# A float32 transpose through TensorE: when stores are issued, and the order of copies into freed regions

## The chip, the cores and the metric

The kernel runs on one core of a Trainium2 chip. The metric is the device time of one execution in microseconds (us). Every profile shown is that of one execution; times inside it are counted from the start of its span.

## The reference

```
def reference(x):          # x: 8192 x 8192, float32
    return np.transpose(x)
```

268.4 MB are read from HBM and 268.4 MB are written to it.

## The kernel before

**Tiling.** The input is cut into two stripes of 4096 columns, and each stripe into 64 chunks of 128 rows: `chunks` has T = 128 entries (s, c), stripe by stripe. A chunk is one load of 2 MB (128 rows x 4096 floats) into one of NIN = 3 input buffers `in`. TensorE turns a chunk into 32 transposed tiles of 128x128, in eight groups q = 0 to 7 of four tiles. The groups 0 to 3 go to one half of PSUM (four banks, `pss[0]`), 4 to 7 to the other (`pss[1]`), so that the whole PSUM holds one chunk. ScalarE (ACT, e = 0) copies the first half to SBUF, VectorE (DVE, e = 1) the second.

**Windows and regions.** The copies go into `regs`, which has NREG = 9 regions of 2 MB. A group q gathers in one region the tiles of up to W = 8 successive chunks, so that a row of the output gets 8 x 128 floats, 4 KB, in one piece. This is the group's window. The windows are staggered: in each chunk one group's window closes (q = c mod 8), and its region is stored by one DMA (2 MB in the middle of the run, less at the start and the end; two pieces where a window spans the change of stripes). Eight windows are open, and one region is spare: a group that closed in chunk t opens its next window in chunk t+1, in the region that was freed by the store of chunk t-1. That store must have landed before the first copy into it.

**Semaphores.** TensorE waits for `s_ld` of its input buffer to come to 18 (line 113): 16 from the load's landing and one from each copying engine, `go`, which says that its half of PSUM has been emptied. It adds one to `s_pe` after every second group, four times a chunk. NH = 4 is the number of groups in a half. `s_st[r]` counts the landed stores of region r, and `s_cp[e]` the copies that closed a window.

**Order of the work around the change.** The queues are in order and the program of each engine is written out for all 128 chunks (TensorE has a loop). For a chunk t ScalarE's program is, before: for each run of groups that one instruction can copy, a wait for `s_pe` (line 222) and the copy (line 223); where a group opens a window in a region that was used before, a wait for `s_st` of that region stands ahead of all copies of the half (line 197); behind a copy that closes a window, a wait for `s_cp` and the store (`store`, lines 151 to 173, called at line 236). Stores of VectorE's half are issued by ScalarE too, behind its own copies, and wait for VectorE's `s_cp`. At last ScalarE waits until TensorE has finished chunk t and issues the load of chunk t+3 into the buffer that chunk t leaves free (lines 237 and 238). So all loads but the first three, and all stores, stand in ScalarE's one DMA queue, in the order store of t, load of t+3, store of t+1, load of t+4. The first three loads are issued by SyncE at the start.

The lines around the change, before:

```
nc.scalar.wait_ge(s_cp[e], count)                 # store: own copy done
...
if stored[r]:
    eng.wait_ge(s_st[r], 16 * stored[r])          # ahead of all copies of the half
...
if t + NIN < T:
    nc.scalar.wait_ge(s_pe, (t + 1) * NR // 2)    # TensorE done with chunk t
    load(t + NIN)
```

Of the kernel before, what the change touches and what calls it, by code (L numbers as in the profile page):

```python
# [40 lines left out]
def kernel(  # L41
# [13 lines left out]
    nc = tc.nc  # L55
# [8 lines left out]
    NR = S // B  # L64
# [5 lines left out]
    with tc.tile_critical():  # L70
        nc.alloc_sbuf_tensor("pad", [P, 32], dt)
        ident = nc.alloc_sbuf_tensor("ident", [P, P], dt).ap()
        ins = [nc.alloc_sbuf_tensor(f"in{k}", [P, J], dt).ap() for k in range(NIN)]
        SIZE = B * W * P
        regs = nc.alloc_sbuf_tensor("regs", [P, NREG * SIZE], dt).ap()
        NH = NR // 2
        pss = [nc.alloc_psum_tensor(f"ps{k}", [P, NH * B * P], dt).ap() for k in range(2)]

        s_id = nc.alloc_semaphore("s_id")
        s_ld = [nc.alloc_semaphore(f"s_ld{k}") for k in range(NIN)]  # L80
        s_st = [nc.alloc_semaphore(f"s_st{k}") for k in range(NREG)]
        s_pe = nc.alloc_semaphore("s_pe")
        s_cp = [nc.alloc_semaphore("s_cpa"), nc.alloc_semaphore("s_cpv")]

        nc.gpsimd.memset(ident, 0.0).then_inc(s_id, 1)  # L85
        nc.gpsimd.wait_ge(s_id, 1)
        nc.gpsimd.affine_select(  # L87
            out=ident,
            in_=ident,
            compare_op=mybir.AluOpType.not_equal,  # L90
            fill=1.0,
            base=0,
            pattern=[[-1, P]],
            channel_multiplier=1,
        ).then_inc(s_id, 1)
        nc.vector.sem_inc(s_ld[0], 1)
        nc.scalar.sem_inc(s_ld[0], 1)

        chunks = [(s, c) for s in range(M // J) for c in range(CH)]

        def load(t):
            s, c = chunks[t]
            (nc.sync if t < NIN else nc.scalar).dma_start(
                out=ins[t % NIN], in_=x[c * P:(c + 1) * P, s * J:(s + 1) * J]
            ).then_inc(s_ld[t % NIN], 16)

        def transposes(k):
            nc.tensor.sem_inc(s_ld[k], -18).wait_op(s_ld[k], 18, "sem-ge")  # L113
            for q in range(NR):
                e, g = divmod(q, NH)
                for b in range(B):
                    tr = nc.tensor.transpose(  # L117
                        pss[e][:, (g * B + b) * P:(g * B + b + 1) * P],
                        ins[k][:, q * B * P + b:(q + 1) * B * P - B + b + 1:B],
                        ident,  # L120
                    )
                if q % 2:
                    tr.then_inc(s_pe, 1)

        T = len(chunks)
        assert T % NIN == NIN - 1
        pe = [nc.tensor.engine]
        nc.tensor.wait_ge(s_id, 2)

        turn = nc.alloc_registers("turn", engines=pe)  # L130
        nc.regs_mov(turn, 0)
        nc.br("turns", engines=pe)
        with nc.body("turns", valid_engines=pe):
            now = nc.snap(turn, min_val=0, max_val=T // NIN)
            with nc.tensor.If(now > 0):
                transposes(NIN - 1)
            for k in range(NIN - 1):
                transposes(k)
            nc.regs_alu(turn, turn, 1, op=mybir.AluOpType.add)
            nc.tensor.br_lt(turn, T // NIN + 1, on_true="turns", on_false="done")  # L140
        nc.switch_bb("done")

        for t in range(NIN):
            load(t)

        copied = [0, 0]
        free = list(range(NREG))
        stored = [0] * NREG
        window = {}

        def store(q, e, count):
            t0, r, parts = window.pop(q)
            nc.scalar.wait_ge(s_cp[e], count)
            base = 0
            pieces = []
            for s, a, z in parts:
                rows = (z - a) * P
                j0 = s * J + q * B * P
                dst = out[j0:j0 + B * P, a * P:a * P + rows]
                dst = dst.rearrange("(q b) i -> q b i", q=P)  # L160
                src = regs[:, r * SIZE + base:r * SIZE + base + B * rows]
                base += B * rows
                pieces.append((rows, dst, src))
            for rows, dst, src in sorted(pieces, key=lambda v: -v[0]):
                if any(stored):
                    st = wide_dma(nc, nc.scalar, "qActDynamicHW", dst, src)
                else:
                    st = nc.scalar.dma_start(
                        out=dst, in_=src.rearrange("q (b i) -> q b i", b=B)
                    )  # L170
                st.then_inc(s_st[r], 16)
                stored[r] += 1
            free.append(r)

        def closes(w, t):
            t0, r, parts = w
            return t + 1 == t0 + sum(z - a for _, a, z in parts)

        for t, (s, c) in enumerate(chunks):
            for e in range(2):  # L180
                eng = (nc.scalar, nc.vector)[e]
                go = s_ld[(t + 1) % NIN]

                place = []
                for q in range(e * NH, (e + 1) * NH):
                    if q not in window:

                        span = (q - c) % W + 1  # L190
                        r = free.pop(0)
                        parts = [(s, c, min(c + span, CH))]
                        if c + span > CH and t + span < T:
                            parts.append((s + 1, 0, c + span - CH))
                        window[q] = (t, r, parts)
                        if stored[r]:
                            eng.wait_ge(s_st[r], 16 * stored[r])
                    t0, r, parts = window[q]
                    k = [p[0] for p in parts].index(s)
                    base = r * SIZE + B * P * sum(z - a for _, a, z in parts[:k])  # L200
                    _, a, z = parts[k]
                    place.append((base + (c - a) * P, (z - a) * P))

                runs = []
                for g in range(NH):
                    if runs:
                        u = runs[-1]
                        gap = place[g][0] - place[g - 1][0]
                        if place[g][1] == place[u[0]][1] and abs(gap) < 2 ** 15 and (
                            len(u) == 1 or gap == place[u[1]][0] - place[u[0]][0]  # L210
                        ):
                            u.append(g)
                            continue
                    runs.append([g])
                for u in runs:
                    off, dist = place[u[0]]
                    gap = place[u[-1]][0] - place[u[-2]][0] if len(u) > 1 else 0
                    dims = [list(regs.ap[0]), [gap, len(u)], [dist, B], [1, P]]
                    o = bass.AP(regs.tensor, regs.offset + off, dims)
                    i = pss[e][:, u[0] * B * P:(u[-1] + 1) * B * P]  # L220
                    i = i.rearrange("p (l b i) -> p l b i", b=B, i=P)
                    eng.wait_ge(s_pe, t * NH + (e * NH + u[-1]) // 2 + 1)  # L222
                    cp = nc.scalar.copy(out=o, in_=i) if e == 0 else nc.vector.tensor_copy(out=o, in_=i)  # L223
                    ends = [e * NH + g for g in u if closes(window[e * NH + g], t)]
                    if ends:
                        cp.then_inc(s_cp[e], 1)
                        copied[e] += 1
                    if u is runs[-1]:
                        if ends:
                            eng.wait_ge(s_cp[e], copied[e])  # L230
                            eng.sem_inc(go, 1)
                        else:
                            cp.then_inc(go, 1)
                    for q in ends:
                        store(q, e, copied[e])
            if t + NIN < T:
                nc.scalar.wait_ge(s_pe, (t + 1) * NR // 2)
                load(t + NIN)
        for r in range(NREG):
            nc.sync.wait_ge(s_st[r], 16 * stored[r])  # L240

# [29 lines left out]
```

## Time and profile before

| what | before |
|---|---|
| median of 3 runs | 1262.03 us (1261.98 to 1262.59) |
| profiled execution | 1262.98 us, of which the span is 1261.2 us |
| bytes read and written | 536.9 MB |
| DMA rate from 400 to 600 us | 430 GB/s |
| TensorE, ScalarE, VectorE busy | 59%, 20%, 24% |
| ACT-issued loads | 125, median 21.7 us from issue to landing |
| full stores | 114 of 2 MB, median 17.5 us from issue to landing |

The span runs from the first to the last instruction; the profiled execution took 1.8 us more than its span, and 0.95 us more than the median. "q10" is the DMA queue of ScalarE, "q1" that of SyncE, "q14" and "q8" carry instructions. A name with a small q behind an engine (ACTq, SPq, PEq) is that engine's sequencer: it issues a DMA or waits. In the table of windows the columns are the stretch and its length, then busy time and number of instructions of PE, PEld, DVE, ACT and POOL, then the granted TensorE clock, the DMA engines' share and the GB/s that they moved.

### The profile page before, as it was taken

The page shows a single profiled execution, that of the slowest core. Times are in us where ns is not written, and L with a number is a line of the kernel's source. Part 1 is how long each engine was busy: PE and PEld are TensorE (multiplying, and loading weights), DVE is VectorE, ACT ScalarE, POOL GpSimd, SP SyncE. Part 2 cuts the span into 40 slices and gives each one's busy share as a digit, 9 for nine tenths or more (in the row PEclk, how much of TensorE's full clock was granted, in tenths as well). Part 3 has the DMA queues.
Part 4 walks back from the last instruction along what each step waited for, and adds up shares of the span by engine and source line. Part 5 has one row for each costly group of instructions (what it writes and reads, how often), then busy time and mean ns, then how long its engine had stood idle before and what let it go on. Part 6 is the DMA issues. An engine that isn't in the chain of part 4 may idle for free. (4 is left out here: it accounts for less than half of the span.)

```text
span 1261.2 us, 9538 instructions
## 1 busy us (share of the span) xinstructions
PE 741.5 (59%) x4096; PEld 720.8 (57%) x4096; DVE 302.5 (24%) x250; ACT 252.8 (20%) x257; POOL 0.7 (0%) x6
## 2 busy tenths in 40 slices
PE   5665655656565655665566555656556555656561
PEld 5565655656565655665565555655556555655551
DVE  2322222222222222223222222222222222222220
ACT  3212121121111211122211221221111211121120
POOL 0000000000000000000000000000000000000000
PEclk9878677777868686777767777686777777686775
DMA  9999999999999999999999999999999999999998
GB/s 380 427 424 427 429 428 429 429 428 430 431 430 429 430 430 429 430 430 430 428 422 427 429 431 429 430 430 429 429 430 431 428 430 430 429 429 431 429 429 351
DMA packets 39273, 536.97 MB, mean 426 GB/s; under 512 B 4320, under 2 KB 4832, under 8 KB 6240
## 3 DMA queue, kind: packets, MB, share of 16 engines
q10 hardware_dynamic: 38832, 530.60, 98.9%
q1 hardware_dynamic: 432, 6.29, 1.2%
q14 instruction: 8, 0.07, 0.0%
q8 instruction: 1, 0.02, 0.0%
HBM read 268.44 MB, written 268.44 MB: 426 GB/s over the span
## 5 line engine op out<-in xcount | busy, mean ns | idle before, releaser
L117 PE MATMUL ps<-ident,in 128*128 128x128 f32 x4096 | 741.5, 363 | 492.6 <-PEq L113 492.6
L117 PEld LDWEIGHTS ps<-ident,in 128*128 128x128 f32 x4096 | 720.8, 220 | 513.0 <-issue 513.0
L223 DVE COPY regs<-ps 128x512 f32<-128x512 f32 (+3 forms) x250 | 302.5, 1246 | 933.1 <-PE ps L117 760.0
L223 ACT COPY regs<-ps 128x512 f32<-128x512 f32 (+3 forms) x256 | 251.5, 1015 | 980.5 <-PE ps L117 489.8
L223 ACT ACT_TABLE_LOAD x1 | 1.3, 1283 | 1.0 <-SPq L70 1.0
L87 POOL TENSOR_SCALAR_AFFINE_SELECT ident<-ident 128x128 f32<-128x128 f32 x1 | 0.3, 292 | 0.2 <-POOL ident L85 0.2
L85 POOL MEMSET ident<- 128x128 f32 x1 | 0.2, 204 | 0.5 <-SPq L70 0.5
L255 POOL MEMSET const-bfloat16-1.0<- 128x1 bf16 x1 | 0.1, 101 | 0.0
L255 POOL MEMSET const-uint8-127<- 128x1 uint8 x1 | 0.1, 101 | 0.0
L255 POOL MEMSET const-float32-0.0<- 128x1 f32 x1 | 0.1, 98 | 0.2 <-issue 0.2
L255 POOL MEMSET const-float32-1.0<- 128x1 f32 x1 | 0.1, 98 | 0.0
## 6 DMA issues: line engine op xcount, KB each, us to landing
in<-in_x_dram ACTq DMA_DIRECT2D x125, 2048.0 KB, 21.7
out_dram<-regs ACTq DMA_DIRECT2D x114, 2048.0 KB, 17.5
out_dram<-regs ACTq DMA_DIRECT2D x4, 1792.0 KB, 15.9
in<-in_x_dram SPq DMA_DIRECT2D x3, 2048.0 KB, 11.8
out_dram<-regs ACTq DMA_DIRECT2D x4, 1536.0 KB, 14.2
out_dram<-regs ACTq DMA_DIRECT2D x4, 1280.0 KB, 15.1
out_dram<-regs ACTq DMA_DIRECT2D x4, 1024.0 KB, 15.5
out_dram<-regs ACTq DMA_DIRECT2D x4, 768.0 KB, 17.8
```

Source lines behind the costliest of these rows:

```text
L85: nc.gpsimd.memset(ident, 0.0).then_inc(s_id, 1)
L87: nc.gpsimd.affine_select(out=ident, in_=ident, compare_op=mybir.AluOpType.not_equal, fill=1.0, base=0, pattern=[[-1, P]], channel_multipl ...
L117: tr = nc.tensor.transpose(pss[e][:, (g * B + b) * P:(g * B + b + 1) * P], ins[k][:, q * B * P + b:(q + 1) * B * P - B + b + 1:B], ident,)
L223: cp = nc.scalar.copy(out=o, in_=i) if e == 0 else nc.vector.tensor_copy(out=o, in_=i)
L255: nc = _bacc.Bacc("TRN2", target_bir_lowering=False, num_devices=1)
```

## The change

A store no longer waits for the copy that closed its window. It waits until TensorE has finished the first two groups of the next chunk (`s_pe` at (t+1)·4 + 1); TensorE begins that chunk only after both engines have signalled `go`, so all copies of chunk t are done then. All stores of a chunk are collected in `closed` and issued there, and the load of chunk t+3 is issued behind them. In the last chunk the old wait stays. Within a half, the copies into a region that was used before go last, and only they wait for the region's store; the first of the others then waits for all groups of the half. Waits for a value of `s_pe` that the engine has already waited for are left out, and `go` is raised by the last copy itself. There are 129 semaphore instructions fewer. The order of the DMAs in ScalarE's queue stays the same but for the last chunk, where the 256 KB store changes places with the last 2 MB store.

```diff
-        def store(q, e, count):
+        def store(q, e, t):
             t0, r, parts = window.pop(q)
-            nc.scalar.wait_ge(s_cp[e], count)
+            if t + 1 < T:
+                nc.scalar.wait_ge(s_pe, (t + 1) * NH + 1)
+            else:
+                nc.scalar.wait_ge(s_cp[e], copied[e])
...
+            closed = []
...
                         if stored[r]:
-                            eng.wait_ge(s_st[r], 16 * stored[r])
+                            fresh[q - e * NH] = (s_st[r], 16 * stored[r])
...
+                runs = sorted(runs, key=lambda u: any(g in fresh for g in u))
+                seen = t * NH + e * NH // 2
...
-                    eng.wait_ge(s_pe, t * NH + (e * NH + u[-1]) // 2 + 1)
+                    need = t * NH + (e * NH + u[-1]) // 2 + 1
+                    if u is runs[0] and len(runs) > 1 and any(g in fresh for g in runs[-1]):
+                        need = t * NH + (e * NH + max(v[-1] for v in runs)) // 2 + 1
+                    if need > seen:
+                        eng.wait_ge(s_pe, need)
+                        seen = need
+                    for sem, value in [fresh[g] for g in u if g in fresh]:
+                        eng.wait_ge(sem, value)
...
-                    if ends:
+                    if t + 1 == T:
                         cp.then_inc(s_cp[e], 1)
                         copied[e] += 1
+                        for q in ends:
+                            store(q, e, t)
+                        continue
                     if u is runs[-1]:
-                        if ends:
-                            eng.wait_ge(s_cp[e], copied[e])
-                            eng.sem_inc(go, 1)
-                        else:
-                            cp.then_inc(go, 1)
-                    for q in ends:
-                        store(q, e, copied[e])
+                        cp.then_inc(go, 1)
+                    closed += [(q, e) for q in ends]
             if t + NIN < T:
-                nc.scalar.wait_ge(s_pe, (t + 1) * NR // 2)
+                if not closed:
+                    nc.scalar.wait_ge(s_pe, (t + 1) * NH)
+                for q, e in closed:
+                    store(q, e, t)
                 load(t + NIN)
+            elif t + 1 < T:
+                for q, e in closed:
+                    store(q, e, t)
```

More of the change, by code (lines that the diff above doesn't have):

```diff
@@ L184 @@
                 place = []
+                fresh = {}
                 for q in range(e * NH, (e + 1) * NH):
```

## The prediction

> **What bounds the kernel now.** I read the page first, then the waits, then the timeline of three places: the start, one stretch in the middle, the end. The page says that the DMA engines have no time to spare:
>
> ```profile
> span 1261.2 us, 9538 instructions
> ...
> DMA  9999999999999999999999999999999999999998
> GB/s 380 427 424 427 429 428 429 429 428 430 431 430 429 430 430 429 430 430 430 428 422 427 429 431 429 430 430 429 429 430 431 428 430 430 429 429 431 429 429 351
> ```
>
> The rate is flat near 430 GB/s but for the first and last of the forty slices. 536.9 MB at 430 GB/s are 1248.6 us of the 1261.2, so any gain within this rate is below 12.6 us, and most of that is the unavoidable start and end. The engines wait for the transfers, as the waits say:
>
> ```profile
> PE ps L117 <- PEq L113: 492.6, 128, 8.5
> ...
> ACT regs L223 <- DMA out_dram<-regs: 479.2, 60, 10.5
> DVE regs L223 <- DMA out_dram<-regs: 173.0, 25, 7.6
> ```
>
> TensorE stands 492.6 us at line 113, 3.8 us a chunk. The 652 us for which the copying engines stand before a region that is still being stored look like the prize of this change, but they lie beside a full DMA queue. The middle of the run, in the timeline:
>
> ```profile
> 608.48 0.55 ACTq L28 DMA_DIRECT2D out_dram<-regs  x1
> 609.06 0.68 ACTq L103 DMA_DIRECT2D in<-in_x_dram  x1
> 610.86 5.41 PEld L117 LDWEIGHTS ps<-ident,in 128*128 128x128 f32 x32 [4.36 <-issue]
> 610.89 5.57 PE L117 MATMUL ps<-ident,in 128*128 128x128 f32 x32 [4.20 <-PEq L113]
> 612.41 0.59 ACT L223 COPY regs<-ps 128x512 f32<-128x512 f32 x1 [6.64 <-PE ps L117]
> ```
>
> The chunk before began at 601.12, so chunks are 9.77 us apart, and a load and a store of 2 MB (4.19 MB) at 430 GB/s take 9.75: the period is the transfers'. A load lands 21.7 us after its issue (page, median), more than two periods, so the queue is two chunks deep.
>
> **The change in the steady part.** Call L the time at which TensorE begins chunk t+1 (load landed, `go` given). Before, the store and the load behind chunk t are issued 2 to 6 us before L or earlier (608.48 and 609.06, L being 610.89). After, both wait for TensorE's first two groups: 1.5 us after L at 610.89 to 612.41, 2.0 us at a slow granted clock (1227.81 to 1229.80). I add the store's issue, 0.55 us, or 1.2 where it has two pieces, and the load's, 0.3 to 0.7. So the load is issued at about L + 3.0. What has been queued ahead of it and not moved at L is the store of t-1 and the load of t+2, 9.75 us of work. The first packet after an issue takes about 1.0 us (next part), so the new work is there at L + 2.5 to L + 4.0, and the queue has 5.75 us or more left: no period grows. The load's time to landing should fall from 21.7 to about 2·9.75 - 3 = 16.5 us, and that is only the queue becoming shallower.
>
> Behind ScalarE's new wait stand the store's and the load's issues and then the copies of chunk t+1. They would start at L + 3 instead of L + 1.5, or L + 6.5 if the load's issue still takes the 3.7 us seen at the change of stripes (min, median and max of its 125 issues: 334, 651 and 4758 ns); with 1.9 us of copies they end by L + 8.4. VectorE's half, where it now waits for all groups, starts when TensorE ends (L + 5.6, at the slow clock L + 6.5) and takes 2.5 us: L + 9.0. Both are before the next L at 9.75, by 0.7 us at worst; should one be late by 0.5 us, TensorE starts late by that and the queue still has over 5 us. The copies into freed regions wait for a store that lands some 4.9 us after L, as now, since the queue's order is the same; that they go last takes other copies out from behind that wait. Worth: 0, because TensorE's next start is set by the load.
>
> The 129 semaphore instructions lie on ScalarE and VectorE, which idle for 980 and 933 us: 0. Their code is fetched by DMA: the page has eight packets on q14, 0.07 MB, so 8.8 KB each; on one of 16 engines (27 GB/s) such a packet takes 0.3 us. At most one falls away, which is worth 0 to -0.3 us; I take -0.1.
>
> **The change at the start.** Here the queue is not yet deep:
>
> ```profile
> 0.94 1.32 SPq L103 DMA_DIRECT2D in<-in_x_dram  x3
> ...
> 8.48 6.55 PE L117 MATMUL ps<-ident,in 128*128 128x128 f32 x32 [8.48 <-PEq L113]
> ...
> 11.09 0.65 ACTq L168 DMA_DIRECT2D out_dram<-regs  x1
> ...
> 15.07 0.36 ACTq L103 DMA_DIRECT2D in<-in_x_dram  x1
> ...
> 16.52 4.08 PE L117 MATMUL ps<-ident,in 128*128 128x128 f32 x32 [1.48 <-PEq L113]
> 17.75 1.07 ACT L223 COPY regs<-ps 128x512 f32<-128x512 f32 x2 [4.41 <-PE ps L117]
> ```
>
> The second of the three first loads is issued at 1.4 and lands 11.8 us later (page, median of the three), at 13.2; the third, 4.9 us of work behind it, lands at 18.1, and its last bytes are in flight until about 17.6. Before, the store of chunk 0 and the fourth load have been issued at 11.09 and 15.07, so the next packets follow at once. After, both wait for chunk 1's first two groups: 17.75, when ScalarE's first copy of that chunk starts now. Chunk 1 itself cannot begin earlier, since it follows VectorE's last copy of chunk 0. So the queue runs dry at 17.6 and gets its next issue at 17.75.
>
> How long from an issue to the first packet in an empty queue the trace shows once, at its very start: SyncE issues at 0.94, and in the windows nothing moves until 1.9:
>
> ```profile
> 0.90:1.90 1.00, 0.00 (x0) 0.00 (x0) 0.00 (x0) 0.92 (x1) 0.50 (x2) 1.00 0.00 0
> 1.90:2.40 0.50, 0.00 (x0) 0.00 (x0) 0.00 (x0) 0.36 (x1) 0.00 (x0) 1.00 1.78 360
> ```
>
> That is 1.0 us, and then the rate needs a while: from 2 to 4 us it is 279 GB/s, which loses 0.7 us against 430. A store into an empty queue is in no row. Bounds: from below 1.0 + 0.15 = 1.1 us lost, if the rate is full at once; from above the whole fixed part of the first load, which was issued at 0.94 and let TensorE start at 8.48, 7.5 us for 4.9 us of bytes, so 2.6 us with the landing's own delay, and 2.75 lost. No gain is possible there: bytes that do not move then must move later, and nothing later has room. I take 1.6, the first packet and over half of the slow rise, because the queue has been warm.
>
> The Trainium skill, "DMA: Bandwidth & Descriptors", section "Latency and other measured facts", gives about 600 ns to the first byte of such a DMA; the trace has 1.0 us. By the page's figure the sum would be 0.4 us lower.
>
> The next chunks do not add to it: the fourth load and the small store would end near 25, and the second store is issued at TensorE's third chunk plus 1.3 (22.30 + 1.3 = 23.6), its packets at 24.6. From there TensorE's chunks come every 5.8 us (22.30, 28.11, 33.93), faster than 4.9 us of load plus the growing stores, and the queue fills.
>
> **The end.** The last chunk starts at 1227.81. The store of chunk 126, issued at 1225.65 now, goes to 1229.8, with packets at 1230.8; ahead of it is the store of chunk 125, 4.9 us of work until 1232.6. Covered by 1.8 us. The stores of the last chunk are issued some 0.6 us later, behind 9.8 us of work. 0.
>
> **Sum.** 1.6 - 0.1 = +1.5 us on the profiled execution, 1262.98 to 1264.5; the median of before is 0.95 us below that execution, so 1262.03 + 1.5 = 1263.5. A measurement of this kernel can tell about 0.2%, 2.5 us, from no change: within 1259.5 and 1264.55 it is the same. My forecast is in that band.
>
> **The rivals.** *Slower, by the start alone:* the refill at 17.75 costs its upper bound, 2.75 us, and 1264.8 or more; it decides from 2.6 us of lost DMA time on. For it: the store of chunk 0 is made of the smallest pieces (512 B) and goes first. Against it: 1.0 us of the 2.6 is landing, which a queue with more work behind hides. 0.24.
>
> *Slower, in every chunk:* the DMA engines do not finish together. At the end their share falls slowly (424 GB/s from 1250 to 1255, then 164 and 57 in two stretches of 2 us), so that some are about 4 us ahead of the last. For these the 9.75 us of queued work at L are 5.75, against 4.0 for the slowest issue. If leading engines ran dry and the others could not use the room, 0.1 us a chunk would be 12 us, 1275; it decides once the load's issue is later than L + 5. Against it: the last engine sets the end, and it has its full 9.75. The same page of the Trainium skill, "Rules for kernel authors", speaks for this rival: it advises to issue a DMA early, so that its fixed cost is covered. 0.06.
>
> *Faster:* the shallow queue keeps the engines together and the tail after 1255 shrinks by its mean loss, (1 - 0.39)·2 + (1 - 0.14)·2 = 2.9 us, and one fetch less lands on the last engine; with the start at its lower bound that is 1262.03 + 1.1 - 2.9 - 0.3 = 1259.9, and a little less is needed to show. 0.07.
>
> *The change does nothing at the start,* because the third load or the clock is later than read: 1262.0. It is inside the band.
>
> **How the numbers follow.** Forecast with the last case 0.63; slower 0.24 + 0.06 = 0.30; faster 0.07. The likeliest alone spans 1261.9 (nothing lost, one fetch less) to 1264.5. For 8 in 10 I reach up past the start's bound to 1266.3 and down to 1260.8, leaving out the steady rival and the faster one.
>
> **What would show it.** Right: fourth load issued near 18.4 instead of 15.07; GB/s between 17.5 and 20 down by 1.2 to 2 us of full rate; chunk period still 9.75; loads' median to landing about 16.5 us; waits of ScalarE and VectorE for stores down by hundreds of us with no gain. Wrong: a second dip of GB/s between 24 and 60 us, middle slices under 428, or a shorter tail after 1255.

## The result, and the profile after

| | before | after |
|---|---|---|
| median of 18 runs each | 1262.51 us (1261.13 to 1263.39) | 1265.57 us (1263.99 to 1269.22) |
| ratio | | 1.0024, 95% interval 1.0018 to 1.0030 |
| profiled execution, of which the span | 1262.98, 1261.2 | 1264.22, 1262.4 |

The kernel is slower by 3.1 us, 0.24%, just over the 0.2% that the prediction took for the least difference it could tell; the interval begins a little below it. The forecast, 1263.5, was "the same"; what came is, by its number, the first rival, slower by the start alone, which had 0.24. The range held the time. The profiled execution is one of the quicker ones of the changed kernel, so the page alone shows less loss (1.2 us) than the medians. The ratios below leave out the runs that took over 1.5% longer than the quickest of their kernel; there are three, one each of e10, e11 and e12.

The page of after, in the same lines as before:

```profile
span 1262.4 us, 9355 instructions
...
DMA  9999999999999999999999999999999999999999
GB/s 363 401 426 430 431 430 427 431 431 428 429 431 429 428 430 430 429 429 431 429 419 427 430 427 432 430 428 430 430 427 430 430 429 429 431 428 430 428 429 377
...
in<-in_x_dram ACTq DMA_DIRECT2D x125, 2048.0 KB, 16.8
out_dram<-regs ACTq DMA_DIRECT2D x114, 2048.0 KB, 12.6
```

The first two slices fell from 380 and 427 GB/s to 363 and 401; from the third to the last but one the row stays within 4 GB/s of what it was, and the last slice rose from 351 to 377. Loads land 16.8 us after their issue instead of 21.7 and stores 12.6 instead of 17.5: the queue is half a chunk shallower, and that changes nothing in the middle. The waits, two lines of before and then those of after:

```profile
DVE regs L223 <- PE ps L117: 760.0, 115, 13.9
ACT regs L223 <- PE ps L117: 489.8, 101, 8.6
```
```profile
DVE regs L237 <- PE ps L117: 935.9, 136, 13.2
ACT regs L237 <- PE ps L117: 748.3, 101, 9.0
...
PE ps L117 <- PEq L113: 490.9, 128, 8.3
ACT regs L237 <- issue: 149.0, 20, 8.5
ACT regs L237 <- DMA out_dram<-regs: 81.1, 32, 8.6
```

The copying engines' waits for stores went from 652 us to 81. It came back as waits for TensorE, 1249.8 us before and 1684.2 after, and as 149.0 us of ScalarE that the profile puts to no wait ("issue"; 2.7 before). TensorE still stands 490.9 us before its loads. The start, in the timeline of ScalarE and in windows (columns as before):

```profile
17.08 0.64 ACTq L171 DMA_DIRECT2D out_dram<-regs  x1
17.76 0.63 ACTq L103 DMA_DIRECT2D in<-in_x_dram  x1
18.44 2.05 ACT L237 COPY regs<-ps 128x512 f32<-128x512 f32 x4 [5.32 <-PE ps L117]
22.89 0.59 ACTq L28 DMA_DIRECT2D out_dram<-regs  x1
23.52 0.61 ACTq L103 DMA_DIRECT2D in<-in_x_dram  x1
```
```profile
17.00:18.00 1.00, 1.00 (x11) 1.00 (x10) 0.00 (x0) 0.00 (x0) 0.00 (x0) 1.00 0.01 0
18.00:20.00 2.00, 1.95 (x17) 1.76 (x15) 0.98 (x2) 1.56 (x4) 0.00 (x0) 1.00 1.04 261
20.00:22.00 2.00, 0.35 (x3) 0.38 (x4) 1.51 (x3) 0.49 (x1) 0.00 (x0) 1.00 0.91 354
...
36.00:38.00 2.00, 1.37 (x12) 1.17 (x10) 1.56 (x3) 1.65 (x2) 0.00 (x0) 1.00 1.22 369
38.00:40.00 2.00, 0.00 (x0) 0.00 (x0) 0.92 (x2) 0.00 (x0) 0.00 (x0) 0.92 0.73 303
60.00:62.00 2.00, 2.00 (x19) 2.00 (x19) 0.00 (x0) 1.24 (x2) 0.00 (x0) 1.00 1.10 385
62.00:64.00 2.00, 0.39 (x4) 0.20 (x2) 1.57 (x2) 0.69 (x1) 0.00 (x0) 1.00 0.86 268
```

The hole is where it was predicted: the first store and the fourth load leave at 17.08 and 17.76 instead of 11.09 and 15.07, no packet of data begins between 17 and 18 us, and the rate is back only after 22. But there are dips at 36 to 40 and 60 to 64 us too, which were not predicted (before has 397, 471, 422 and 432 GB/s in the same four stretches). One number sums it up, the mean rate of the first 80 us, first before, then after:

```profile
0.00:80.00 80.00, 48.61 (x320) 47.00 (x320) 23.80 (x31) 21.61 (x28) 0.70 (x6) 0.89 0.98 408
```
```profile
0.00:80.00 80.00, 47.71 (x313) 46.29 (x314) 21.97 (x30) 20.18 (x27) 0.70 (x6) 0.90 0.97 391
```

(408 - 391) · 80 / 430 = 3.2 us of full rate. That this is also the difference of the medians is in part chance, since the rest of an execution varies too.

In this one the end, from 1200 us on, lost 1.9 us of full rate less (from the trace's packets), the tail being shorter, and the stretch from 80 to 1200 us lost as much as before, so the end moved by 1.2 us only. The last stretches, first before, then after:

```profile
1255.00:1257.00 2.00, 0.00 (x0) 0.00 (x0) 0.00 (x0) 0.00 (x0) 0.00 (x0) 0.50 0.39 164
1257.00:1259.00 2.00, 0.00 (x0) 0.00 (x0) 0.00 (x0) 0.00 (x0) 0.00 (x0) 0.50 0.14 57
```
```profile
1255.00:1257.00 2.00, 0.00 (x0) 0.00 (x0) 0.00 (x0) 0.00 (x0) 0.00 (x0) 0.50 0.96 410
1257.00:1259.00 2.00, 0.00 (x0) 0.00 (x0) 0.00 (x0) 0.00 (x0) 0.00 (x0) 0.50 0.96 406
1259.00:1261.00 2.00, 0.00 (x0) 0.00 (x0) 0.00 (x0) 0.00 (x0) 0.00 (x0) 0.50 0.39 143
```

### The profile page after: what moved, and what is told of

Read it like the earlier page. It is cut to its first block, busy times and chain, and to the rows that moved or that the text cites. A ratio compares the mean times of both kernels' runs of the same rounds, so it can differ in the third digit from the quotient of the medians.

```text
span 1262.4 us, 9355 instructions
## 1 busy us (share of the span) xinstructions
PE 744.5 (59%) x4096; PEld 723.8 (57%) x4096; DVE 302.0 (24%) x250; ACT 252.8 (20%) x257; POOL 0.7 (0%) x6
## 5 line engine op out<-in xcount | busy, mean ns | idle before, releaser
L117 PE MATMUL ps<-ident,in 128*128 128x128 f32 x4096 | 744.5, 364 | 490.9 <-PEq L113 490.9
## 6 DMA issues: line engine op xcount, KB each, us to landing
in<-in_x_dram ACTq DMA_DIRECT2D x125, 2048.0 KB, 16.8
out_dram<-regs ACTq DMA_DIRECT2D x114, 2048.0 KB, 12.6
```

Of the source, the lines that this page charges most:

```text
L117: tr = nc.tensor.transpose(pss[e][:, (g * B + b) * P:(g * B + b + 1) * P], ins[k][:, q * B * P + b:(q + 1) * B * P - B + b + 1:B], ident,)
```

## The experiments

Each kernel is the changed one with a helper `early(t)`. Where it is true, chunk t takes the old order: a store behind its own copy, the load when TensorE has finished the chunk. The copies into freed regions go last in all of them. Ratios are against the kernel before, run on the same chip in the same batch; "lost" is (408 - rate of the first 80 us) · 80 / 430. Medians are those of all runs; the GB/s and "lost" are of one profiled execution each, which for e10 is its quickest (1291.88 us).

| kernel | median us | ratio (95% interval) | GB/s, 0 to 80 us | lost us | GB/s, 200 to 600 us |
|---|---|---|---|---|---|
| after_again: the change | 1266.75 | 1.0035 (1.0023 to 1.0047) | 391 | 3.2 | 427 |
| e1: old order in chunks 0 to 7 | 1262.48 | 1.0003 (0.9994 to 1.0012) | 408 | 0.0 | 429 |
| e2: old order in chunk 0 | 1264.97 | 1.0026 (1.0015 to 1.0036) | 389 | 3.5 | 429 |
| e5: new order in chunks 0 to 7 alone | 1265.19 | 1.0022 (1.0012 to 1.0032) | 390 | 3.3 | 430 |
| e3: old order throughout | 1262.59 | 0.9996 (0.9987 to 1.0005) | 408 | 0.0 | 430 |
| e8: old order in chunks 0 to 2 | 1263.25 | 1.0011 (1.0000 to 1.0022) | 406 | 0.4 | 429 |
| e14: old stores, new loads | 1263.45 | 1.0008 (0.9998 to 1.0017) | 402 | 1.1 | 430 |
| e10: e1, waits for four groups | 1308.64 | 1.0323 (1.0261 to 1.0384) | 410 | -0.4 | 419 |
| e9: e1, waits for six groups | 1317.37 | 1.0434 (1.0421 to 1.0448) | 411 | -0.6 | 410 |
| e13: old stores, loads at six groups from chunk 8 | 1262.10 | 0.9996 (0.9982 to 1.0011) | 410 | -0.4 | 430 |
| e11: old order, loads split in two | 1375.1 | 1.0849 (1.0786 to 1.0912) | 236 | | 386 |
| e12: e9 with split loads | 1842.9 | 1.4578 (1.4545 to 1.4611) | 235 | | 296 |

**Start or every chunk.** The edits:

```diff
 def early(t):
-    return False      # the change
+    return t < 8      # e1;   e2: t < 1;   e5: t >= 8
```

> The changed kernel once more, as the yardstick for the others of this batch. Both theories: ratio to the kernel before 1.002 to 1.003, some 1265.5 us; in the profile the DMA rate between 17 and 20 us is about half of 430 GB/s again, and the chunk period from 200 to 600 us is 9.75 us.

> The changed kernel, but the first 8 chunks issue their stores behind their own copies and their loads when TensorE has finished the chunk, as before the change. Theory start (the loss is the queue that runs dry at 17.6 us and what follows in the first 80 us): the loss is gone, ratio to before 0.999 to 1.001, 1261.5 to 1263 us, and no hole in the DMA rate at 17 to 20 us. Rival every chunk (the later issues cost something in each of the other 120 chunks): the loss stays, ratio 1.002 to 1.003.

> As the last one, but only the very first chunk takes the old order. Theory start, as the prediction worked it out (only the first refill is exposed, the second comes in time): ratio to before 0.999 to 1.001. Rival within the start (the dips at 30 to 32, 37 to 39 and 60 to 65 us of the changed kernel also come from the late issues of chunks 1 to 7): about half of the loss stays, ratio 1.001 to 1.002. Rival every chunk: ratio 1.002 to 1.003.

> The reverse: only the first 8 chunks have the new waits, the other chunks issue as before the change; copies into freed regions go last throughout. Theory start: the whole loss is here, ratio to before 1.002 to 1.003, 1265 us or so. Rival every chunk: ratio 1.000 to 1.001.

e1 and e5 split the change in time and agree: the new order in the first eight chunks has the loss, and in the other 120 the ratio shows none. (Together they have 1.0025, the change in the same batch 1.0035, whose interval begins at 1.0023.) e2 contradicts the prediction's own step. With chunk 0 put right the hole at 17 us is gone, and just as much is lost later, more than either reading of the start had expected. Four stretches before, then the same of e2:

```profile
0.00:20.00 20.00, 10.04 (x61) 9.91 (x62) 2.81 (x5) 5.03 (x9) 0.70 (x6) 1.00 0.91 369
20.00:40.00 20.00, 13.18 (x103) 12.54 (x103) 9.61 (x16) 6.82 (x11) 0.00 (x0) 1.00 1.02 416
40.00:60.00 20.00, 13.71 (x96) 13.37 (x95) 4.91 (x7) 6.08 (x6) 0.00 (x0) 0.83 1.00 423
60.00:80.00 20.00, 11.68 (x66) 11.19 (x64) 6.46 (x4) 3.69 (x4) 0.00 (x0) 0.74 1.01 424
```
```profile
0.00:20.00 20.00, 9.92 (x64) 9.75 (x64) 3.25 (x6) 5.49 (x9) 0.70 (x6) 1.00 0.91 367
20.00:40.00 20.00, 12.49 (x98) 11.85 (x96) 9.17 (x15) 5.97 (x9) 0.00 (x0) 1.00 0.95 372
40.00:60.00 20.00, 12.62 (x73) 12.33 (x74) 4.91 (x7) 3.85 (x4) 0.00 (x0) 0.74 1.01 400
60.00:80.00 20.00, 11.57 (x75) 11.24 (x74) 4.65 (x3) 3.96 (x5) 0.00 (x0) 0.86 1.01 415
```

The loss moved from the first line to the second (44 GB/s over 20 us are 2.0 us), the third (1.1 us) and the fourth (0.4 us): the fifth load is still issued some 3 us late (23.73 instead of 20.63), and the bytes ahead of it now end sooner.

**How long the start is, and what in it costs.** e3 and e8 change `early` to `True` and `t < 3`; e14 has `early` true and

```diff
 if not closed:
-    nc.scalar.wait_ge(s_pe, (t + 1) * NH)
+    nc.scalar.wait_ge(s_pe, (t + 1) * NH + 1)     # the load alone waits for the next chunk
```

> All chunks issue stores and loads as before the change; only the copies into freed regions go last, and repeated waits are left out. All theories: the order of the copies is worth nothing, since TensorE's next start is set by the load: ratio to before 0.999 to 1.001, with ScalarE's and VectorE's waits for stores cut from 652 us to under 250. If the order itself were what costs: 1.002.

> The changed kernel with the old order in the first three chunks. Theory of the queue's start, refined by the run with one old chunk (there the dry time moved from 17 to 23 us and stayed as long, since the fifth load was still issued some 3 us late): once the loads of chunks 0 to 2 are early, the DMAs of chunk 3 are issued near 35 us and the bytes ahead of them last to 37, so nothing runs dry: ratio 1.000 to 1.0012. Rival (the loss comes from the slow packets that go with a shallow queue, wherever it is shallow): 1.002 or more, with dips between 45 and 70 us.

> All stores are issued as before the change, from the first chunk on; all loads wait for two groups of the next chunk, as with the change. In the steady part the run with late loads alone lost nothing even at six groups, so what is seen here is the start. Theory load: the fourth and fifth loads are issued some 3 us late as in the changed kernel, and the small early stores cannot fill the hole at 17 to 20 us: ratio 1.0015 to 1.003. Rival store (it is the stores behind which packets slow down, at the start too): 0.999 to 1.001.

e3: the order of the copies is worth nothing, though the copying engines' waits for stores fell to 77 us there. e8: with three chunks put right most of the loss is gone, as the bytes ahead of the fourth chunk's DMAs predicted; 0.4 us of rate stays, with a dip to 315 GB/s at 44 to 46 us, of the kind that the rival expected from 45 us on, and the ratio's interval reaches from 1.0000 to 1.0022. The ratio of e14, 1.0008, lies in the rival's range, and its interval reaches up to 1.0017 into the other's, so the time does not decide. The rates of its profiled execution say where the two parts of the change cost:

```profile
0.00:20.00 20.00, 9.87 (x61) 9.74 (x62) 2.89 (x5) 4.72 (x8) 0.70 (x6) 1.00 0.88 344
20.00:40.00 20.00, 12.83 (x101) 12.16 (x99) 9.53 (x16) 7.02 (x11) 0.00 (x0) 1.00 1.00 403
40.00:60.00 20.00, 14.63 (x95) 14.34 (x96) 4.90 (x7) 6.08 (x6) 0.00 (x0) 0.83 1.01 429
60.00:80.00 20.00, 11.22 (x67) 10.70 (x65) 4.80 (x4) 3.96 (x4) 0.00 (x0) 0.83 1.01 430
```

The late loads alone make the hole before 40 us (25 and 13 GB/s under before, 1.8 us). The later dips are absent, also those at 36 to 40 us (426 and 406 GB/s there): they come with the late stores. The packets say the same. Of those of 16 KB that begin between 26 and 80 us, 43 take over 0.9 us with the change, 35 in after_again, 43 in e2, 36 in e5 and 25 in e8; with early stores it is 9 before, 9 in e3, 16 in e1 and 5 in e14. The usual time is 0.61 us. Late stores with early loads were not run, so the stores' part is known from this difference alone.

**How far the steady part is from harm.**

```diff
-    nc.scalar.wait_ge(s_pe, (t + 1) * NH + 1)     # e1, from chunk 8 on
+    nc.scalar.wait_ge(s_pe, (t + 1) * NH + 3)     # e9;   e10: + 2
```

> Old order in the first 8 chunks; from there on stores and loads wait for six groups of the next chunk instead of two, some 3 us later again (load issued about 5.5 to 6.5 us after that chunk's start, packets 1.3 us later). If only the last DMA engine counts, its 9.75 us of queued work still cover this: ratio 1.000 to 1.0015, and the engines' landings come closer together, under 3 us. If engines that are ahead must not run dry (rival every chunk), they do here when they are over 2 us ahead: 1.005 or more, period over 9.80 us.

> Old order in the first 8 chunks, then a wait for four groups of the next chunk: between the change (two groups, near 1.000 with an old start) and the run with six groups (1.043, with a DMA share of 1.01 all the while and packets that take twice as long at the ends of stores). Theory ahead (a packet slows where too little is queued behind its own DMA; with six groups that is so for every engine at the end of each store): the new DMAs are there at L + 4.7, the last engine ends its store at L + 4.9 and the leading ones earlier, so only engines that are ahead slow down: 1.002 to 1.015. Rival (the loss is proportional to the delay): about 1.02.

The prediction gave the queue 5.75 us to spare. The first two more groups cost some 41 us by the ratio. After the chunk's start the store leaves at 2.0 us with the change (least 1.2, most 2.6), at 3.7 in e10 (2.7 to 4.3) and at 5.2 in e9 (4.4 to 6.0), and the load some 0.6 us behind it: 2.6, 4.3 (4.9 at most) and 5.7 (all medians over chunks 12 to 119). The runs of e10 lie far apart, 1291.88 to 1316.83 us. The DMA engines' share in the middle of the run shows no idle time in either, e10 first, then e9 with one of its dips:

```profile
200.00:600.00 400.00, 233.62 (x1280) 227.17 (x1280) 94.73 (x73) 76.53 (x69) 0.00 (x0) 0.75 1.01 419
```
```profile
200.00:600.00 400.00, 239.04 (x1250) 232.61 (x1248) 91.93 (x71) 74.26 (x63) 0.00 (x0) 0.67 1.01 410
502.00:504.00 2.00, 2.00 (x12) 2.00 (x10) 0.00 (x0) 0.00 (x0) 0.00 (x0) 0.50 0.97 279
```

The share is 1.01, as at 430 GB/s; the packets themselves take longer. In the dip of 502 to 504 us 15 packets at the end of a store take 1.1 to 1.2 us instead of 0.61 (read from the trace's packets). From 200 to 600 us 246 packets of 16 KB take over 0.9 us in e10 and 502 in e9, most of them at the end of a store, against 6 before and 3 with the change. Both expectations of e10 are missed: the loss is larger than either, and not proportional to the delay.

**Load or store.** e13 has `early` true, and only the load waits:

```diff
-    nc.scalar.wait_ge(s_pe, (t + 1) * NH)
+    nc.scalar.wait_ge(s_pe, (t + 1) * NH + (3 if t >= 8 else 0))
```

> Stores are issued as before the change, only the loads (from chunk 8 on) wait for six groups of the next chunk. At the end of a store there is then a load and the next store queued behind it, as with the change. Theory ahead (count or bytes): little loss, under 1.01. Rival (a late load is what costs, whatever the stores do): 1.03 to 1.045.

```profile
200.00:600.00 400.00, 241.20 (x1312) 234.58 (x1312) 96.73 (x77) 79.62 (x73) 0.00 (x0) 0.74 1.01 430
```

The load waits for the same six groups as in e9 and leaves 4.7 us after the chunk's start (4.3 to 5.4; it has no store's issue ahead of it), later than in e10, and it costs nothing while the stores leave early (5 packets over 0.9 us). So in the steady part it is the store's time that matters, and the change moved it to within one step of the edge.

**What the slow packets depend on.** One reading is that a store must find more than one DMA queued behind it when it ends. The split loads were to test it:

```diff
-    dma_start(out=ins[t % NIN], in_=x[c * P:(c + 1) * P, ...])
+    for h in range(0, P, P // 2):
+        dma_start(out=ins[t % NIN][h:h + P // 2, :], in_=x[c * P + h:c * P + h + P // 2, ...])
```

(`s_ld` then counts to 34.)

> The yardstick for the next one: old order throughout, each load cut into two DMAs of 64 partitions. All theories: 1.000 to 1.01, from twice as many issues and ends of DMAs.

> Six groups' wait after an old start, with each load cut into two DMAs of 64 partitions. Theory count (what matters is how many DMAs are queued behind the one that ends): two are queued now at the end of a store where one was, and the loss against the split yardstick goes, ratio under 1.01. Rival bytes (what matters is how much is queued, or the time of the issue): the loss stays, 1.04.

The yardstick failed: with split loads alone the rate is low for the first 400 us and nearly full from then on, though the kernel does the same all the time (e11, slices of 34 us):

```profile
GB/s 208 252 278 323 298 299 320 314 328 354 404 390 426 425 425 430 429 428 429 428 431 423 418 426 428 427 429 428 431 430 429 429 428 428 427 428 430 429 427 351
```

What makes it so is not shown, and this is no clean test. What can be read is that with two DMAs behind each store the late wait still costs, by more than before: 1.4578 / 1.0849 = 1.34. From 700 to 1200 us, where e11 has 427 GB/s, e12 has 291. This speaks against the number of queued DMAs as what is missing; it does not settle it.

## Why the prediction was right and wrong

**What bounds it: right.** From the third slice on the rate is 430 GB/s before and after, and removing 571 us of waits for stores (652 to 81; 77 in e3, ratio 0.9996) moved nothing.

**The steady part: right in its number, wrong in its reason.** Predicted 0; e1 has 1.0003 (0.9994 to 1.0012). The chunk period is 9.76 us before and after (median). The load's time to landing was predicted as 16.5 us and is 16.8. But the step "the queue has 5.75 us or more left" took a queue that is not empty for a queue that runs at full pace. The second rival had "it decides once the load's issue is later than L + 5"; the runs show harm with the load at L + 4.3 (e10), by the store's delay and not by the load's, and with the DMA engines' share still at 1.01. In e13 the load leaves at up to L + 5.4 without harm. The advice in the Trainium skill that was set beside that rival ("DMA: Bandwidth & Descriptors", section "Rules for kernel authors": issue a DMA early, so that its fixed cost is covered) agrees with the stores' sign (e10, 1.0323) and does not show for the loads (e13, 0.9996). Its reason does not account for e10, where a whole load, 4.9 us of work, is still queued to cover the store's start. One reading of the prediction was off without harm to the sum: before the change loads left 0.2 to 4.2 us before L, not "2 to 6 us or earlier".

The margin is so thin that single executions cross it. In after_again the rate from 200 to 600 us was 427 instead of 430, 400 · 3 / 430 = 2.8 us, with 70 packets over 0.9 us instead of 3, and its span 1267.3 us. Against before, that execution lost the same 3.2 us in the first 80 us, 5.0 us more from 80 to 1200, and 2.0 us less behind that (from the trace's packets). This may be why the changed kernel's runs spread over 5.2 us and those of before over 2.3; one execution is not enough to show it.

**The start: the mechanism right, its size half.** The hole and its two causes (late issue, time to the first packet) are there. Of its two steps the first was near and the second failed:

- *The first refill*, 1.6 us: from 16 to 26 us the windows show 339, 458, 426, 254 and 475 GB/s before and 254, 261, 354, 426 and 393 after, 264 GB/s less in sum over stretches of 2 us, which is 1.2 us. In after_again and e5, whose start has the same waits, the same stretch lost 2.2 and 2.3 us; their first store left later, at 17.68 and 17.54. The term was near. The first packet came 1.3 us after the issue began (17.08 to 18.38, from the trace's packets); on SyncE it was 1.0 (0.94 to 1.97). The 0.6 us that the Trainium skill gives ("DMA: Bandwidth & Descriptors", section "Latency and other measured facts") is met if it is counted from the end of the issuing instruction: 0.66 us in both (17.72 to 18.38, 1.31 to 1.97).
- *"The next chunks do not add to it"* is the step that failed. It checked that nothing runs dry a second time once the first refill has come late. It did not ask what the chunks would lose without that delay (e2: as much again), nor what late stores do while the queue is shallow (the dips at 36 to 40 and 60 to 64 us, gone in e14). These are the rest of the 3.2 us: 2.0 in this execution, 1.0 in after_again and e5.

So the upper bound of the start, 2.75 us, was nearly what came, and that is in part luck: it was meant for the first load's whole fixed part in one refill, and the refill took 1.2 to 2.3 us with the chunks behind it adding the rest, the next two above all (e8).

**The end: right that nothing is lost.** The tail even got shorter, as the third rival had it: the 16 completions of the last store lie 1.1 us apart, where they were 4.6 us apart before. This goes with the late stores: it is 1.1 to 1.7 us in after, after_again, e1, e2 and e8, and 3.4 to 4.6 in before, e3, e5, e13 and e14. But it is no gain by itself. In e2 and e8 the stores landing between 1150 and 1230 us still have 4.9 and 4.3 us between first and last completion, so that there the engines ahead lost their lead only before the last stores, and the end is set by the last engine. The prediction's "covered by 1.8 us" was worked out for the last engine alone. The tail did not decide the sign.

**Instructions: -0.1.** The instruction packets on q14 went from eight to six, not by one at most, and the profile has 183 instructions fewer, not 129: semaphore instructions of ScalarE (93) and VectorE (90). No run here can show the worth of that.

**The signs.** All that was named for "right" came: the fourth load at 17.76, 17.5 to 20 us down from 420 to 209 GB/s (1.2 us of full rate), the period, the landing time and the waits. Of those named for "wrong" two came as well, a second dip before 60 us and a shorter tail. The third, middle slices under 428, tells nothing, since before has such slices too.

**Sum.** 1.5 us was forecast, 3.1 came; in the medians the difference has the size of what the start lost beyond its first term.

## What to carry to other kernels

Before moving an issue later because a queue is deep, look at the stretch in which it is not yet deep: this change cost nothing that the ratio shows in 120 chunks and 3 us in the first eight. When one late transfer is put right, work out the next late one behind it before calling the first the cause, for a closed loop of loads loses its slack once, and repairing one link only moves the place. And a DMA share of 1.0 does not say that the engines run at full pace: read the GB/s beside it, and move a wait by one more step to learn how far the edge is.

## What the runs showed of the hardware

- With the DMA engines' share at 1.01, the rate was 430, 419 and 410 GB/s as stores left 2.0, 3.7 and 5.2 us after the chunk's start (medians of after, e10, e9); packets at the end of a store then took up to twice their 0.61 us. The running store lands 4.8 us after the chunk's start on the last engine. A store that reaches the engines after that, 1.3 us behind its issue, leaves only a load behind the running one. This fits the last engine in these three kernels and in e13. It is not the whole of it: in after and e1 some 10 and 13 of the 16 engines end the running store before the next one reaches them (an estimate from the store's 16 completions and the 1.3 us), and only 3 and 9 packets slowed. What slows them is not shown.
- Loads of 2 MB cut into two DMAs of 64 partitions each ran at 208 to 404 GB/s in the first 400 us (e11, by slices) and at 427 from 700 to 1200 us, where whole loads have 430 both from 200 to 600 and there. With late stores besides (e12) the rate was 296 and 291 in these two stretches. Why is not shown.
- The 16 completions of one DMA lie up to 4.9 us apart at the end of the run before, and 0.4 to 0.6 us apart at its start (from the trace's semaphore updates). With the change they lie 2.3 us apart from 1150 to 1230 us, and 1.1 at the last store.
